# A second buffer for spilled S5 output matrices, and a ring of six instead of seven for the state input matrices

## The chip, the cores and the metric

The kernel runs on one core of one Trainium2 chip. Of that core's engines the text speaks of TensorE (PE in the profile, with PEld for its weight loads), VectorE (DVE), ScalarE (ACT), GpSimd (POOL) and SyncE (SP, which only issues DMAs here), and of its 16 DMA engines. The metric is the device time of one execution in microseconds; lower is better. 1.0 of a granted TensorE clock is 2.4 GHz, 0.5 is 1.2 GHz.

## The reference

One inference step of a trunk of four layers (S5, retention, Hyena, S5) at model width 1024, over 128 context tokens and 256 latent tokens (384 columns, T in the kernel). The part around the change is layer 0, a bidirectional S5 layer: 1024 channels in 64 groups of 16, each group driving one 64-dimensional complex diagonal state.

```python
proj = h @ w_in
u, gate = proj[..., :S5_WIDTH], proj[..., S5_WIDTH:]
for d in range(2):                       # both directions
    ab = exp(lam * dt)                   # complex, per state
    bu = einsum('blgh,gph->blgp', ud, bb)        # bb = f(lam, dt) * b
    h_t = ab * h_{t-1} + bu_t                    # associative scan
    yd = Re(einsum('blgp,ghp->blgh', h, c))
    y = y + yd
g = gelu(y + d_skip * u)
y = g * sigmoid(g @ w_glu + b_glu)
out = (y * silu(gate)) @ w_out
```

## The kernel before

**Chunked scan.** The scan is done in chunks of Q = 8 tokens. For every group and direction the kernel builds matrices from lam, b and c: a state input matrix (eight tokens of u into the state at the end of the chunk), a Toeplitz matrix (u to y inside the chunk), and an output matrix CP (state at the chunk's start into the eight y). Only the recurrence over 48 chunks is then sequential (`recur`, lines 770 to 799, on VectorE).

**Half blocks and blocks.** The 64 groups are sixteen half blocks hb of four groups; block b is the half blocks 2b and 2b+1 (128 channels). For layer 0 everything is generated in the kernel:

- `gen_b1` (line 642): loads b and c (`bc`, two half blocks a load), and on VectorE makes for each direction BP = F1 x b + FI x b' (`expand`, lines 626 to 636: two multiplies and an add, lines 631, 632 and 636). ScalarE then changes the sign of c in place (line 651).
- `gen_b2` (line 660): TensorE multiplies c with BP (line 668, the Toeplitz part, into a PSUM bank), and transposes BP (line 674, two PSUM banks). ScalarE copies the transposes to the tile PB (line 675), which is the transposed state input matrix of the half block, and the Toeplitz part to Kc (lines 677 to 680), which a DMA puts into HBM.
- `use_p(b)` (line 743, step P): TensorE multiplies U of the block with PB of its two half blocks (line 749); ScalarE copies to Ss (one buffer, line 751), TensorE transposes (line 758), ScalarE writes the chunk inputs X (line 761). With that the two PB buffers are free again.

All of these use the four PSUM banks of `psm`.

**Spilled output matrices.** CP of a half block is needed only later, behind the recurrence. Ten of the sixteen are generated there (`gen_c`). Six, hb in `SPL` = 4, 6, 8, 10, 12, 14, are generated early, in `gen_b1`, and spilled to HBM: for each direction VectorE writes CP (line 631) and the second product `xt` (line 632, tag `xs`, two buffers, so one half block's worth); an accumulating DMA adds `xt` to CP (line 634, issued by POOL); and when both have landed a DMA stores CP to `cpd` (line 650, on POOL's queue too). CP has one buffer of 4 KB per partition.

**Order.** The string PLAN0 gives the program order: A n generates half blocks until n exist, U n multiplies a slab of the input projection (two blocks of U), P n is `use_p`, T is a background unit (a slab of the modulation weights `mod_w`, 1 MB each), R0 and R1 are the recurrences of the first and second half of the blocks. R0 needs P0 to P3, R1 needs P4 to P7.

```python
PLAN0 = "A7 U0 T1 U1 T1 P0 A9 T1 P1 A11 T1 U2 T1 P2 A13 T1 P3 A15 T1 R0 U3 T1 P4 T1 A16 P5 T1 T1 P6 P7 R1"
```

The order that each engine really gets is fixed when the kernel is built: the framework lists instructions by their place in the program, simulates the engines, and issues on each the first one that is ready in its simulation. A tile that has no free buffer is not ready. So a number of buffers changes not only waits on the chip, but also the order in which instructions stand on the engines. On the chip each engine keeps that order.

**Behind it.** The gate half of the input projection (`dense`, line 141 matmuls, eight blocks) is held behind the last matmul of P7 (`issue_after(mark[0].ins)`). SP's queue also loads the Toeplitz matrices back (`Tt`, line 852). Pools are stacked, and when the pools of the generation are closed, the tiles of the next stage take their place: a new tile waits for the old tiles at the same addresses. Seven PB buffers lie at the start of that space; `sgate` covers the first three, the two `Tt` buffers the fourth and the fifth.

Of the kernel before, what the change touches and what calls it, by code (L numbers as in the profile page):

```python
# [10 lines left out]
F32 = mybir.dt.float32  # L11
# [20 lines left out]
LINE = 520  # L32
EHY = 2048
SPLIT = True
RB = 7
NBC = 2
NH = 2
RB1 = 10
# [69 lines left out]
def hybrid_trunk(ctx: ExitStack, tc: tile.TileContext, I, O, dbg=None, layers=(0, 1, 2, 3)):  # L108
# [518 lines left out]
    def expand(out, rot, T1, T2, x, sl, l0, bufs, eng, add, tag="xt"):  # L627
        c1 = T1[:, sl, l0:l0 + 4].rearrange("p e l -> p l e").unsqueeze(3).to_broadcast([128, 4, 8, 16])
        c2 = T2[:, sl, l0:l0 + 4].rearrange("p e l -> p l e").unsqueeze(3).to_broadcast([128, 4, 8, 16])
        t = rot.tile([128, 4, 8, 16], F32, tag=tag, name="xt", bufs=bufs)  # L630
        eng.tensor_tensor(out, c1, x[:, 0].unsqueeze(2).to_broadcast([128, 4, 8, 16]), op=OP.mult)  # L631
        eng.tensor_tensor(t, c2, x[:, 1].unsqueeze(2).to_broadcast([128, 4, 8, 16]), op=OP.mult)  # L632
        if add is None:
            nc.gpsimd.dma_start(out, t, accum_op=OP.add)
        else:
            add.tensor_tensor(out, out, t, op=OP.add)  # L636

    def expand_c(CP, rot, tb, xc, hb, xb, eng, add, tag="xt"):
        for d in range(2):
            expand(CP[:, d], rot, tb["B1"], tb["BI"], xc[:, d], slice(1, 9) if d == 0 else slice(8, 0, -1), d * 64 + hb * 4, xb, eng, add, tag)  # L640

    def gen_b1(j, hb, tb, rot, xb=1, nb=1, spill=False):
        if hb % nb == 0:
            tb["bc"] = rot.tile([128, nb, 2, 2, 2, 4, 16], F32, tag="bc", name="bc", bufs=2)
            (nc.gpsimd if hb > 2 else nc.sync).dma_start(tb["bc"], I["s5bc"][j, hb // 4, :, hb % 4:hb % 4 + nb])
        rb, xc = tb["bc"][:, hb % nb, 0], tb["bc"][:, hb % nb, 1]
        if spill:
            CP = rot.tile([128, 2, 4, 8, 16], F32, tag="CP", name="CP", bufs=1)
            expand_c(CP, rot, tb, xc, hb, 2, V, None, "xs")
            getattr(nc, SPQ).dma_start(I["cpd"][hb], CP.rearrange("p d g e c -> p (d g e c)"))  # L650
        S.activation(xc, xc, AF.Copy, scale=tb["sgn"][:, 1:2])
        BPs = []
        for d in range(2):
            BP = rot.tile([128, 4, 8, 16], F32, tag="BP", name="BP", bufs=2 if j else 3)
            expand(BP, rot, tb["F1"], tb["FI"], rb[:, d], slice(7, None, -1) if d == 0 else slice(0, 8), d * 64 + hb * 4, xb, V, G if j else V)
            BPs.append(BP)
        return BPs, xc
# [28 lines left out]

    def gen_c(j, hb, tb, rot, CP, xb, eng=V, add=G):
        xc = rot.tile([128, 2, 2, 4, 16], F32, tag="xc", name="xc")
        nc.sync.dma_start(xc, I["s5bc"][j, hb // 4, :, hb % 4, 1])
        expand_c(CP, rot, tb, xc, hb, xb, eng, add)  # L690

# [9 lines left out]
    def s5(i, j, nxt, begun=lambda: None):  # L701
        def mk(st, name, bufs=1, **kw):
            return st.enter_context(tc.tile_pool(name=f"{name}_{i}", bufs=bufs, reuse_waits="tile", **kw))
# [23 lines left out]
        eP = ExitStack()  # L727
        ring = mk(eP, "s5b", RB if j == 0 else RB1)
        ru = mk(eP, "s5a", 2)
# [5 lines left out]
        def get_p(hb):  # L735
            if j == 0:
                PBs[hb] = gen_b2(j, hb, tb, grot, gen_b1(j, hb, tb, grot, nb=NBC, spill=hb in SPL), ring)
            else:
                PBs[hb] = ring.tile([128, 4, 2, 128], F32, tag="PB", name="PB")
                PQ.dma_start(PBs[hb].rearrange("p g d c -> p (g d c)"), I["pbd"][hb])  # L740
# [194 lines left out]
    def retention(i, zpool, hpool, nxt):  # L935
# [44 lines left out]
        if True:  # L980
            todo = []
            grot = es.enter_context(tc.tile_pool(name="retgr", bufs=1, reuse_waits="tile"))
            tb = GEN[1]
            ops = {}

            def both(hb):
                if hb > 0:
                    gen_b2(1, hb - 1, tb, grot, ops.pop(hb - 1))
                if hb < 16:
                    ops[hb] = gen_b1(1, hb, tb, grot, xb=1)  # L990
                    gen_cs(1, hb, tb, grot)
            todo += [lambda hb=hb: both(hb) for hb in range(17)] + list(bg)
            bg.clear()
            for k, f in enumerate(todo):
                while len(bg) < S0 + k * (SLOTS - S0) // len(todo):
                    bg.append(lambda: None)
                bg.append(f)
# [580 lines left out]
```

## Time and profile before

| | us |
|---|---|
| runs shown | 1636.39, 1632.05, 1635.85 |
| their median | 1635.85 |
| profiled execution, its time | 1632.28 |
| profiled execution, its span | 1630.5 |
| mean granted TensorE clock | 0.951 |

| engine | busy us | share of the span |
|---|---|---|
| PE | 1449.2 | 89% |
| DVE | 1246.0 | 76% |
| ACT | 692.2 | 42% |
| POOL | 664.3 | 41% |

The span is the time from the first to the last instruction of the profiled execution; 1.8 us of its time lie around it. A share of busy time is a mean over stages; stages of S5 in layer 0 (to about 350 us), where TensorE has gaps, are read for themselves. A line of a timeline gives the start, the duration, the engine, the line in the code, the operation, output <- inputs, the count, and in brackets the idle time of the engine just before it, with what ended it.

### The profile page before, as it was taken

The page shows a single profiled execution, that of the slowest core. Times are in us where ns is not written, and L with a number is a line of the kernel's source. Part 1 is how long each engine was busy: PE and PEld are TensorE (multiplying, and loading weights), DVE is VectorE, ACT ScalarE, POOL GpSimd, SP SyncE. Part 2 cuts the span into 40 slices and gives each one's busy share as a digit, 9 for nine tenths or more (in the row PEclk, how much of TensorE's full clock was granted, in tenths as well). Part 3 has the DMA queues.
Part 4 walks back from the last instruction along what each step waited for, and adds up shares of the span by engine and source line. Part 5 has one row for each costly group of instructions (what it writes and reads, how often), then busy time and mean ns, then how long its engine had stood idle before and what let it go on. Part 6 is the DMA issues. An engine that isn't in the chain of part 4 may idle for free. (4 is left out here: it accounts for less than half of the span.)

```text
span 1630.5 us, 27608 instructions
## 1 busy us (share of the span) xinstructions
PE 1449.2 (89%) x10370; PEld 1280.7 (79%) x10370; DVE 1246.0 (76%) x2935; ACT 692.2 (42%) x1275; POOL 664.3 (41%) x484
## 2 busy tenths in 40 slices
PE   6778787798799899999979999999999999988996
PEld 3555585577588888889968988999998898767886
DVE  8966998699886767755968887888888874379565
ACT  2434522244333333334445544546445534542443
POOL 2111242325374857551225665655666332132221
PEclk9887899899799999999989999999999999999998
DMA  9487499843555555543333322322322345577531
GB/s 359 130 260 224 150 222 253 284 178 128 216 173 179 183 207 187 183 154 130 127 125 101 101 78 75 101 84 95 100 78 94 106 174 201 167 217 196 199 130 65
DMA packets 107805, 261.39 MB, mean 160 GB/s; under 512 B 28535, under 2 KB 68568, under 8 KB 88088
## 3 DMA queue, kind: packets, MB, share of 16 engines
q1 hardware_dynamic: 80768, 200.12, 37.2%
q0 software_dynamic: 11984, 34.87, 7.7%
q10 hardware_dynamic: 14920, 24.65, 4.3%
q8 instruction: 82, 1.34, 0.3%
q14 instruction: 51, 0.42, 0.1%
HBM read 220.37 MB, written 30.83 MB: 154 GB/s over the span
## 5 line engine op out<-in xcount | busy, mean ns | idle before, releaser
L136 POOL TENSOR_TENSOR wl<-wr,wh 128x1024 fp32r<-128x1024 f32 (+2 forms) x99 | 248.9, 2515 | 300.2 <-ACT wh L164 273.6
L164 ACT CAST wh<-wr 128x1024 fp32r<-128x1024 f32 (+4 forms) x211 | 215.7, 1028 | 315.0 <-PE psd L141 200.5
L141 PE MATMUL psd<-hh,wh 128*128 128x384 f32 x880 | 307.3, 350 | 13.5 <-DVE X L798 7.0
L141 PE MATMUL psd<-hl,wh 128*128 128x384 f32 x880 | 305.7, 347 | 6.4 <-DVE hl L472 6.2
L141 PE MATMUL psd<-hh,wl 128*128 128x384 f32 x880 | 305.3, 347 | 4.7 <-POOL wl L136 2.6
L151 DVE TENSOR_TENSOR wl<-wr,wh 128x1024 fp32r<-128x1024 f32 (+3 forms) x112 | 147.2, 1315 | 71.9 <-ACT wh L164 71.5
L141 PEld LDWEIGHTS psd<-hh,wh 128*128 128x128 f32 x880 | 169.7, 193 | 26.6 <-issue 14.5
L141 PEld LDWEIGHTS psd<-hl,wh 128*128 128x128 f32 x880 | 169.9, 193 | 15.9 <-DVE hl L472 8.9
L141 PEld LDWEIGHTS psd<-hh,wl 128*128 128x128 f32 x880 | 169.7, 193 | 12.2 <-issue 5.1
L141 PE MATMUL psd<-wl,hh 128*128 128x256 f32 x384 | 110.0, 288 | 4.0 <-POOL wl L136 2.0
L141 PE MATMUL psd<-wh,hh 128*128 128x256 f32 x384 | 110.0, 292 | 2.6 <-ACT k L1077 1.6
L141 PE MATMUL psd<-wh,hl 128*128 128x256 f32 x384 | 109.0, 286 | 0.0
L381 PE MATMUL psn<-wr,sgc 128*32 128x256 f32 x640 | 58.3, 460 | 35.0 <-DMA wr<-in_mod_w_dram 23.9
L141 PE MATMUL psd<-zb,wh 128*128 128x384 f32 x240 | 80.9, 338 | 0.0
L141 PEld LDWEIGHTS psd<-wl,hh 128*128 128x128 f32 x384 | 74.1, 193 | 6.3 <-POOL wl L136 3.2
L141 PEld LDWEIGHTS psd<-wh,hh 128*128 128x128 f32 x384 | 73.3, 193 | 4.5 <-ACT k L1077 2.0
L636 POOL TENSOR_TENSOR BP<-BP,xt 128x512 f32<-128x512 f32 x32 | 47.3, 1479 | 71.9 <-DVE xt L632 36.4
L141 PEld LDWEIGHTS psd<-wh,hl 128*128 128x128 f32 x384 | 74.1, 193 | 0.1
L631 DVE TENSOR_TENSOR CP<-B,xc 128x512 f32<-128x512 f32 x52 | 52.9, 1044 | 26.5 <-DMA scratch_cpd_dram<-CP 15.6
L632 DVE TENSOR_TENSOR xt<-BI,xc 128x512 f32<-128x512 f32 x52 | 47.2, 909 | 29.6 <-POOL CP L636 17.2
L381 PEld LDWEIGHTS psn<-wr,sgc 128*32 128x32 f32 x640 | 20.0, 124 | 56.9 <-DMA wr<-in_mod_w_dram 27.8
L797 DVE TENSOR_TENSOR X<-X,m 128x64 f32<-128x64 f32 x184 | 64.2, 349 | 0.0
(385 smaller groups left out, 3843.1 us busy)
## 6 DMA issues: line engine op xcount, KB each, us to landing
wr<-in_mod_w_dram SPq DMA_DIRECT2D x40, 1024.0 KB
wr<-in_hy_w_in_dram SPq DMA_DIRECT2D x32, 1024.0 KB
wr<-in_ret_w_in_dram SPq DMA_DIRECT2D x24, 1024.0 KB
wr<-in_s_w_in_dram SPq DMA_DIRECT2D x16, 1024.0 KB
wm<-in_mod_w_dram SPq DMA_DIRECT2D x8, 1024.0 KB
CP<-xt POOLq DMA_DIRECT2D x32, 256.0 KB, 7.2
Tt<-scratch_kd_dram SPq DMA_DIRECT2D x128, 64.0 KB
wr<-in_s_w_glu_dram SPq DMA_DIRECT2D x8, 1024.0 KB
```

Source lines behind the costliest of these rows:

```text
L136: G.tensor_tensor(out, a, b, op=op)
L141: TE.matmul(out, lhs[a], rhs[b], start=start and i == 0, stop=stop and i == len(combos) - 1)
L151: V.tensor_sub(out, a, b)
L164: S.copy(hi, ap)
L381: TE.matmul(ps[q * 32:(q + 1) * 32, :256], sg[:, kb, 6 - 2 * u:38 - 2 * u], raw[:, kb, :], start=u == 0 and k2 == 0, stop=u == 3 and k2 == 1)
L631: eng.tensor_tensor(out, c1, x[:, 0].unsqueeze(2).to_broadcast([128, 4, 8, 16]), op=OP.mult)
L632: eng.tensor_tensor(t, c2, x[:, 1].unsqueeze(2).to_broadcast([128, 4, 8, 16]), op=OP.mult)
L636: add.tensor_tensor(out, out, t, op=OP.add)
L797: V.tensor_add(dst, dst, m1[:, 0])
```

## The change

It gives the tile CP of the spilled half blocks (in `gen_b1`) two buffers in place of one, and the ring of PB tiles of layer 0 (`RB`, the pool `s5b`) six buffers in place of seven. A CP buffer and a PB buffer are both 4 KB per partition, so that the pools take the same space together. Nothing is computed otherwise; PLAN0, the `xs` pair of buffers and `SPL` stay.

```diff
@@ -32,7 +32,7 @@
 EHY = 2048
 SPLIT = True
-RB = 7
+RB = 6
 NBC = 2
@@ -645,7 +645,7 @@
         if spill:
-            CP = rot.tile([128, 2, 4, 8, 16], F32, tag="CP", name="CP", bufs=1)
+            CP = rot.tile([128, 2, 4, 8, 16], F32, tag="CP", name="CP", bufs=2)
             expand_c(CP, rot, tb, xc, hb, 2, V, None, "xs")
```

`RB` is used once: `ring = mk(eP, "s5b", RB if j == 0 else RB1)`.

## Rows read from the trace of the kernel before

**Rows 1.** The page: span, busy time by engine, and the chain by engine.

```profile
span 1630.5 us, 27608 instructions
PE 1449.2 (89%) x10370; PEld 1280.7 (79%) x10370; DVE 1246.0 (76%) x2935; ACT 692.2 (42%) x1275; POOL 664.3 (41%) x484
...
PE 8%; DVE 4%; ACT 1%; DMA 1%; issue 0%; POOL 0%; DVEq 0%; ACTq 0%; POOLq 0%
```

**Rows 2.** Busy time by stretch: PE, PEld, DVE, ACT, POOL; clock, DMA share, GB/s.

```profile
125.00:135.00 10.00, 10.00 (x80) 7.35 (x78) 7.96 (x14) 3.68 (x9) 0.56 (x1) 0.86 0.84 261
135.00:145.00 10.00, 10.00 (x89) 7.55 (x87) 6.56 (x13) 5.96 (x15) 2.87 (x4) 1.00 0.69 164
145.00:155.00 10.00, 3.56 (x42) 2.30 (x40) 3.54 (x8) 1.04 (x3) 0.52 (x1) 0.66 0.67 204
...
185.00:195.00 10.00, 8.66 (x102) 5.24 (x96) 10.00 (x84) 6.44 (x13) 0.56 (x1) 1.00 0.36 108
195.00:205.00 10.00, 10.00 (x70) 9.17 (x69) 8.03 (x51) 5.16 (x8) 2.25 (x1) 1.00 0.08 18
...
290.00:320.00 30.00, 22.28 (x250) 16.38 (x244) 18.60 (x46) 8.86 (x17) 10.62 (x10) 0.80 1.04 318
...
500.00:1000.00 500.00, 467.37 (x3207) 434.93 (x3206) 370.94 (x650) 219.23 (x427) 253.24 (x173) 0.98 0.43 144
```

**Rows 3.** Instructions of tile CP: its accumulating DMAs' issues, and times to landing.

```profile
L634 POOL DMA_DIRECT2D CP<-xt x32: 850/867/1256, 72.1 to 310.6; - x32
...
DMA to landing us min/median/max: 2.9/7.4/14.1
```

**Rows 4.** Timeline of DVE: the spilled matrices' writes, with the waits before them.

```profile
135.63 1.29 DVE L631 TENSOR_TENSOR CP<-B,bc 128x512 f32<-128x512 f32 x2 [2.54 <-DMA scratch_cpd_dram<-CP]
...
141.14 0.69 DVE L632 TENSOR_TENSOR xt<-BI,bc 128x512 f32<-128x512 f32 x1 [1.54 <-DMA CP<-xt]
...
143.71 0.69 DVE L632 TENSOR_TENSOR xt<-BI,bc 128x512 f32<-128x512 f32 x1 [1.27 <-DMA CP<-xt]
...
153.49 1.29 DVE L631 TENSOR_TENSOR CP<-B,bc 128x512 f32<-128x512 f32 x2 [6.46 <-DMA scratch_cpd_dram<-CP]
...
177.60 1.28 DVE L631 TENSOR_TENSOR CP<-B,bc 128x512 f32<-128x512 f32 x2
```

**Rows 5.** Timeline of PE: the two long waits of this stage.

```profile
156.25 1.94 PE L381 MATMUL psn<-wr,sgc 128*32 128x256 f32 x16 [6.60 <-DVE mod L393]
...
179.47 1.08 PE L668 MATMUL psm<-BP,bc 128*32 128x128 f32 x16 [8.49 <-ACT bc L651]
```

**Rows 6.** Timelines of PE and DVE: step P3, and the starts of R0 and R1.

```profile
162.91 1.95 PE L749 MATMUL psm<-PB,U 128*64 128x256 f32 x16
...
168.95 0.18 DVE L778 COPY XF<-X 128x32 f32<-128x32 f32 x1 [0.55 <-ACT X L761]
...
201.84 0.18 DVE L778 COPY XF<-X 128x32 f32<-128x32 f32 x1 [1.97 <-ACT X L761]
```

**Rows 7.** Timelines of ACT (PB copies of hb 8, 12, 14), PE (P1, P4).

```profile
125.82 0.58 ACT L675 COPY PB<-psm 128x512 f32<-128x512 f32 x1 [0.61 <-PE psm L674]
...
162.58 1.07 ACT L675 COPY PB<-psm 128x512 f32<-128x512 f32 x2 [0.15 <-PE psm L674]
...
181.64 0.58 ACT L675 COPY PB<-psm 128x512 f32<-128x512 f32 x1 [0.61 <-PE psm L674]
...
126.57 1.62 PE L749 MATMUL psm<-PB,U 128*64 128x256 f32 x8
...
182.38 1.95 PE L749 MATMUL psm<-PB,U 128*64 128x256 f32 x16
```

**Rows 8.** Timelines of SP (Toeplitz and weight loads) and PE (P7's second half).

```profile
189.26 5.69 SPq L852 DMA_DIRECT2D Tt<-scratch_kd_dram  x8
206.64 0.34 SPq L155 DMA_DIRECT2D wr<-in_mod_w_dram  x1
...
194.82 1.08 PE L749 MATMUL psm<-PB,U 128*64 128x256 f32 x8
```

## Prediction, made before the result was known

> **What bounds the kernel now.** I first read the page. TensorE is busy 89% of the span, and the chain that ended last has only 8% of PE and 4% of DVE on it, since it reaches back no further than the last layer [rows 1]. It therefore says nothing about layer 0, where the change is, and I follow the waits there by hand.
>
> Next I read the busy time by stretch. In the middle of the kernel PE works 467.37 of 500 us [rows 2]: there a stage that starts earlier ends as much earlier, since the work before its end is fixed. Around 150 us it is otherwise: between 145 and 155 us PE works 3.56 us of 10, DVE 3.54, ACT 1.04, POOL 0.52 [rows 2]. Every engine stands still together, so one wait holds them all. The timeline of DVE names it: at 153.49 the write of a spilled CP had waited 6.46 us for the store of the CP before it [rows 4]. There is one CP buffer, so the next may be written only when the store has read the last. PE's next work had then waited 6.60 us for a DVE instruction that stands behind that write [rows 5]. The same wait, 2.54 us, stands before the write at 135.63 [rows 4]. The other writes show next to none of it.
>
> Then I ask whether that time reaches the end. The half blocks made on DVE feed P3 on PE at 162.91, its X lets R0 start on DVE at 168.95, R1 starts at 201.84 when P7's X is there [rows 6]; the gate's matmuls are held behind P7. Between them DVE is full (10.00 us of 10 from 185 to 195) [rows 2]. So a microsecond that DVE gains before 160 us moves R0, and with it R1 and the gate. The stretch behind, 290 to 320 us, has its DMA engines full (share 1.04), but they do nearly nothing (0.08) between 195 and 205 us [rows 2]: those loads wait for buffers that the gate's matmuls free, so they move forward together with P7.
>
> **The second CP buffer.** It removes the two waits for the store: 2.54 + 6.46 = 9.0 us of DVE time, both before P3 and with no other work of DVE beside them [rows 4]. In their place may come the wait for the `xs` pair, which keeps two buffers: the products of the next spilled half block wait until the accumulating DMAs have read the last ones. This is seen as 1.54 and 1.27 us at 141.14 and 143.71 [rows 4]. But those accumulates were issued behind the CP write at 135.63; if CP is written some 6 us earlier, beside its products, they land earlier too. Bounds: the pair's waits vanish (2.8 us more gain), or they grow until they replace the removed waits (the gain is 0). I take them as they are, 2.8 us, nearest to the rows that show them.
>
> The last spilled matrix, half block 14, is written at 177.60 without a wait, because the order fixed at build time put it there, within R0; PE had then waited 8.49 us for ACT's sign change, which needs that write done [rows 4, 5]. With a free buffer the planner can put it where its products stand, before R0. That lets P4 to P7 end earlier, but R1 also needs R0's end, and R0 is bound by DVE. I count nothing for it; its bound above is the 1.97 us that DVE waited before R1 [rows 6]. No instruction is added: six matrices with their writes, accumulates and stores stay. What moves on POOL's queue is the accumulate's issue, 0.87 us each, two a matrix [rows 3], and the store, which waits in that queue until both have landed; the loads of `bc` stand in that queue too, and would wait 1.7 us for a pair moved ahead of them. They are prefetched a pair of half blocks ahead, which hides that; uncovered it costs 1.7 us.
>
> At one place a rule speaks against this. What the rows show is a DMA share of 0.84 between 125 and 135 us, against 0.69 in the ten microseconds after it, where these accumulates run now [rows 2]; and times to landing of 7.4 us at the median, 14.1 at most [rows 3]. Moved earlier, they go into the fuller stretch. The Trainium skill, page "DMA: Bandwidth & Descriptors", section "Issuing engines are not separate DMA queues", says that DMAs of all issuing engines run on the same 16 engines and interleave. By that rule a second matrix in flight gains no bandwidth of its own, and the result is the second rival below; the rows bear it out only as far as the landing times vary.
>
> **Six PB buffers.** Half block n can now be copied into PB only after the matmuls that read half block n-6, instead of n-7. I lay ACT's copies beside the P steps. Half block 8 is copied at 125.82 and would wait for the first half of P1, which ends at 126.57 + 1.62 = 128.2: 2.4 us. Half block 12 is copied at 162.58 and would wait for P3's first half, 162.91 + 1.95/2 = 163.9: 1.3 us. Half block 14 at 181.64 waits for P4's first half, 182.38 + 1.95/2 = 183.4: 1.7 us [rows 6, 7]. Half block 10 is like half block 12, and the odd ones are copied after the other half, so they don't wait; nor does half block 6, copied after P0's first half. What is queued behind a waiting copy is ACT's own work (Kc, the sign of c, Ss), and two of the four `psm` banks are held meanwhile. The P steps are near the copies, since nothing but the order keeps them back: their U and their PB are there long before. Of the four only half block 12's lies in front of R0, as its two copies may now come between P3's matmuls and P3's Ss. I charge 1.3 us. Bounds: 0, if ACT's order lets Ss go first, and the four waits in full, 4 x 2.4 = 9.6 us.
>
> The six buffers also move what lies over them. `Tt`'s first buffer will lie where the last half blocks were, so its load, now at 189.26, can wait until P7's matmuls are over at 194.82 + 1.08 = 195.9: 6.6 us later [rows 8]. It takes 5.69 us to issue, so it would be done by 201.6, and SP's next load, of `mod_w`, goes out only at 206.64, when a weight buffer comes free [rows 8]. That slack of 5 us hides it, and P7 moves forward besides; without the cover, up to 6.6 us of delay would reach the weight loads queued behind it on SP. I count nothing.
>
> **Sum.** -9.0 + 1.3 = -7.7 us. Against the profiled execution: 1632.28 - 7.7 = 1624.6 us. That execution lies 3.6 us under the median of the runs shown, 1635.85, so I expect a median of 1628.2 us.
>
> **Rivals.** (1) More is gained: the pair's waits go (2.8) and so does the wait before R1 (1.97), and the ring costs nothing: 9.0 + 2.8 + 2.0 = 13.8 us, 1622. For it: the late write at 177.60 held PE for 8.49 us. Against it: R0 has DVE to itself.
> (2) The place of the wait is taken: the second buffer is there, but the `xs` pair holds the next matrix, as two accumulates land in up to 14.1 us and not 7.4. Then 6.7 of the 9.0 us come back, and with the ring's 1.3 the gain is 1.0: 1635, no change. For it: the pair's waits are in the rows already, and the DMA share is high. Against it: the removed wait comes after an accumulate *and* a store, one landing after the other; the pair's waits for the accumulate alone.
> (3) The ring closes, and it is slower. The place is ACT's copy to PB. If the planner makes half blocks 9 us earlier, but leaves P3 and P4 where they are (162.91 and 182.38), then half blocks 12 and 14 each wait 9.0 us more in front of ACT's queue, with two PSUM banks held. This costs 2 x 9.0 against 9.0 gained: 9 us slower, 1645. It decides from the point where P steps move less than the half blocks do; A stands ahead of P in PLAN0, so the order prefers to make half blocks. Against it: P needs nothing but a bank and its turn.
> (4) The new order disturbs a later stage, in either sign; the trace of before can't show it. I let it widen the range by some 3 us.
>
> **How the numbers follow.** Forecast 0.42, rival 1 0.12, rival 2 0.26, rival 3 0.15, rival 4 0.05. A run of this kernel can tell about 0.3% from no change, 4.9 us: faster means below 1631, slower above 1640.8. The forecast and rival 1 are faster but for a tenth of the forecast that ends short: 0.50. Rival 2, that tenth and a part of 4 are the same: 0.32. Rival 3 and the rest are slower: 0.18. Cases of both signs matter; the forecast's own range is 1624 to 1631 (the pair's waits, and the ring at 0 to 4 us). For 8 in 10 I take 1619, which is rival 1 less 3 us, to 1643, which cuts off the upper half of rival 3.
>
> **What would show it.** Right: no wait of DVE for the store of CP; CP and its products side by side; the stretch 145 to 155 us filled; P3, R0 and R1 each some 8 us earlier, and the same distance still there at 500 us. Ring: ACT's copies to PB behind line 749, by 1 to 2 us. Wrong: long waits of line 632 for an accumulate (rival 2); copies to PB that wait several microseconds, with P3 no earlier than 162 (rival 3); or R1 earlier and the end not, which would mean that the stretch at full DMA share gives the gain back.

## The result, and the profile of the changed kernel

| | before | changed |
|---|---|---|
| median, us | 1635.85 | 1647.93 |
| lowest and highest, us | 1630.1 to 1637.31 | 1643.74 to 1655.2 |
| time of the profiled execution, us | 1632.28 | 1647.11 |
| its span, us | 1630.5 | 1645.2 |

The ratio is 1.0086, 95% interval 1.0057 to 1.0116: slower, by about 14 us by that ratio (the two medians differ by 12.1). 1628.2 was forecast, and 1643 was the upper end of the range.

The page of the changed kernel, as [rows 1]: the busy time of every engine is that of before within 5 us. PE's own time for the same 10370 matmuls is 4.6 us longer (its mean granted clock is 0.946, before 0.951); the rest of the 14.7 us of span is time in which it waits.

```profile
span 1645.2 us, 27617 instructions
PE 1453.8 (88%) x10370; PEld 1285.2 (78%) x10370; DVE 1245.1 (76%) x2935; ACT 691.9 (42%) x1275; POOL 662.0 (40%) x484
...
PE 7%; DVE 5%; DMA 1%; ACT 0%; SPq 0%; issue 0%; POOL 0%; DVEq 0%; ACTq 0%; POOLq 0%
```

The same stretches as in [rows 2] (busy us of PE, PEld, DVE, ACT, POOL; granted clock, DMA share, GB/s). Between 145 and 155 us, where every engine had stood still, PE now works 8.21 us and DVE 7.94: that hole is gone. But from 290 to 320 us PE works 16.93 us where it had 22.28.

```profile
125.00:135.00 10.00, 10.00 (x81) 7.52 (x78) 8.37 (x16) 4.75 (x10) 2.74 (x4) 0.93 0.97 269
...
145.00:155.00 10.00, 8.21 (x112) 5.15 (x108) 7.94 (x18) 4.25 (x11) 1.11 (x2) 1.00 0.99 288
...
290.00:320.00 30.00, 16.93 (x158) 12.32 (x159) 19.07 (x40) 6.10 (x10) 11.47 (x11) 0.72 0.92 296
500.00:1000.00 500.00, 467.78 (x3191) 434.44 (x3191) 364.45 (x634) 215.96 (x425) 250.79 (x172) 0.97 0.43 144
```

DVE's timeline, as [rows 4] and [rows 6]: the spilled writes (CP<-B,bc), the starts of R0 and R1 (XF<-X), the first CP of the Y stage (CP<-B,xc) and the last xT of layer 0. No write waits for a store; two wait for the load of `bc` instead. R0 starts 5.2 us earlier than in [rows 6], R1 3.9 us earlier. Then it turns: Y's first CP comes at 235.37 (before: 224.93), and the last xT of layer 0 at 418.83 (before: 412.00). The changed kernel first, then the last two of these for the kernel before.

```profile
126.56 1.29 DVE L631 TENSOR_TENSOR CP<-B,bc 128x512 f32<-128x512 f32 x2
140.27 0.69 DVE L631 TENSOR_TENSOR CP<-B,bc 128x512 f32<-128x512 f32 x1 [3.29 <-DMA bc<-in_s5bc_dram]
...
158.22 0.69 DVE L631 TENSOR_TENSOR CP<-B,bc 128x512 f32<-128x512 f32 x1 [2.48 <-DMA bc<-in_s5bc_dram]
...
163.71 0.18 DVE L778 COPY XF<-X 128x32 f32<-128x32 f32 x1 [1.07 <-ACT X L761]
...
197.93 0.18 DVE L778 COPY XF<-X 128x32 f32<-128x32 f32 x1 [4.19 <-ACT X L761]
...
235.37 0.68 DVE L631 TENSOR_TENSOR CP<-B,xc 128x512 f32<-128x512 f32 x1
...
418.83 0.74 DVE L522 SCALAR_TENSOR_TENSOR xT<-psd,gt,xT 128x128 f32<-128x128 f32 x2 [3.81 <-PE psd L141]
```

```profile
224.93 0.67 DVE L631 TENSOR_TENSOR CP<-B,xc 128x512 f32<-128x512 f32 x1
...
412.00 0.74 DVE L522 SCALAR_TENSOR_TENSOR xT<-psd,gt,xT 128x128 f32<-128x128 f32 x2 [3.81 <-PE psd L141]
```

What stands ahead of that first CP is found on SP's timeline, as [rows 8]. Its input `xc` is loaded at 226.42, behind 32 Tt loads (8 + 5 + 9 + 5 + 5). Before (second fence), it stood behind 16, the 8 of [rows 8] and 3 + 5 more, and was loaded at 214.30.

```profile
192.06 6.15 SPq L852 DMA_DIRECT2D Tt<-scratch_kd_dram  x8
...
203.13 3.20 SPq L852 DMA_DIRECT2D Tt<-scratch_kd_dram  x5
...
210.11 6.59 SPq L852 DMA_DIRECT2D Tt<-scratch_kd_dram  x9
...
217.37 3.49 SPq L852 DMA_DIRECT2D Tt<-scratch_kd_dram  x5
221.47 0.33 SPq L155 DMA_DIRECT2D wr<-in_s_w_in_dram  x1
221.84 4.32 SPq L852 DMA_DIRECT2D Tt<-scratch_kd_dram  x5
226.42 0.85 SPq L689 DMA_DIRECT2D xc<-in_s5bc_dram  x2
```

```profile
207.03 1.82 SPq L852 DMA_DIRECT2D Tt<-scratch_kd_dram  x3
...
209.59 4.39 SPq L852 DMA_DIRECT2D Tt<-scratch_kd_dram  x5
214.30 0.81 SPq L689 DMA_DIRECT2D xc<-in_s5bc_dram  x2
```

### The profile page after: what moved, and what is told of

It is laid out like the page before. It is cut to its first block, busy times and chain, and to the rows that moved or that the text cites. A ratio compares the mean times of both kernels' runs of the same rounds, so it can differ in the third digit from the quotient of the medians.

```text
span 1645.2 us, 27617 instructions
## 1 busy us (share of the span) xinstructions
PE 1453.8 (88%) x10370; PEld 1285.2 (78%) x10370; DVE 1245.1 (76%) x2935; ACT 691.9 (42%) x1275; POOL 662.0 (40%) x484
## 5 line engine op out<-in xcount | busy, mean ns | idle before, releaser
L151 DVE TENSOR_TENSOR wl<-wr,wh 128x1024 fp32r<-128x1024 f32 (+3 forms) x112 | 146.7, 1310 | 70.7 <-ACT wh L164 70.5
L381 PE MATMUL psn<-wr,sgc 128*32 128x256 f32 x640 | 57.1, 446 | 34.5 <-DMA wr<-in_mod_w_dram 30.6
L636 POOL TENSOR_TENSOR BP<-BP,xt 128x512 f32<-128x512 f32 x32 | 47.0, 1470 | 53.4 <-DVE xt L632 22.3
L632 DVE TENSOR_TENSOR xt<-FI,bc 128x512 f32<-128x512 f32 x64 | 49.6, 775 | 19.9 <-POOL BP L636 10.7
L381 PEld LDWEIGHTS psn<-wr,sgc 128*32 128x32 f32 x640 | 19.5, 121 | 55.5 <-DMA wr<-in_mod_w_dram 28.7
```

Of the source, the lines that this page charges most:

```text
L151: V.tensor_sub(out, a, b)
L381: TE.matmul(ps[q * 32:(q + 1) * 32, :256], sg[:, kb, 6 - 2 * u:38 - 2 * u], raw[:, kb, :], start=u == 0 and k2 == 0, stop=u == 3 and k2 == 1)
```

## The experiments

Three theories. **Theory 1**: the time is lost behind R1, in the Y stage (the stage that writes the other CPs and makes y), since the planner's new order puts the `xc` loads behind twice as many Tt loads. **Theory 2**: the smaller ring costs it, since Tt's buffers now lie over the last half blocks' PB. **Theory 3**: any edit gives a new plan, and the later stages come out by chance. Later a question was added about the stage ahead of R1.

One table serves all runs. Each row is a profiled execution, cut at the start of R1, at the start of the last xT of layers 0, 1 and 2, and at the end; all cells but the last two are us of that one execution. "Ratio" is the kernel's time against the kernel before on the same chip, with its interval. The rows were measured on several chips, on which the kernel before had medians from 1631.5 to 1635.9, so kernels are compared by the ratio and not by the median.

| kernel (label) | R0 starts | R1 starts | R1 to end of layer 0 | layer 1 | layer 2 | layer 3 | median us | ratio |
|---|---|---|---|---|---|---|---|---|
| before | 168.9 | 201.8 | 210.2 | 415.8 | 554.8 | 247.9 | 1635.85 | 1 |
| before, again (e5) | 160.9 | 194.1 | 212.2 | 415.2 | 556.0 | 246.5 | | |
| changed | 163.7 | 197.9 | 220.9 | 420.8 | 555.7 | 249.9 | 1647.93 | 1.0086 |
| changed, again (e6) | 165.1 | 200.7 | 220.7 | 418.9 | 555.0 | 249.9 | | |
| ring of six alone (e1) | 176.9 | 209.3 | 211.5 | 417.5 | 555.0 | 247.9 | 1642.63 | 1.0052 (1.0025 to 1.0079) |
| the same, again (e12) | 174.6 | 206.5 | 213.9 | 419.1 | 554.3 | 247.2 | | |
| the same, third (e18) | 172.7 | 205.0 | 214.7 | 417.8 | 555.8 | 249.7 | | |
| changed, pools swapped (e2) | 164.1 | 197.6 | 212.9 | 417.6 | 558.8 | 247.8 | 1644.29 | 1.0069 (1.0036 to 1.0101) |
| the same, again (e7) | 164.7 | 197.7 | 214.0 | 421.4 | 558.6 | 255.2 | | |
| changed, swapped in layer 0 (e11) | 167.9 | 200.6 | 213.3 | 419.6 | 557.9 | 252.8 | 1643.53 | 1.0071 (1.0050 to 1.0092) |
| before, pools swapped (e8) | 173.4 | 207.6 | 218.5 | 417.1 | 558.0 | 254.8 | 1653.39 | 1.0108 (1.0073 to 1.0143) |
| changed, `xc` by ACT (e3) | 166.3 | 199.3 | 215.6 | 419.0 | 557.4 | 248.1 | 1643.37 | 1.0069 (1.0040 to 1.0097) |
| before, `xc` by ACT (e4) | 167.5 | 200.6 | 217.1 | 419.5 | 554.6 | 248.9 | 1641.73 | 1.0050 (1.0021 to 1.0080) |
| changed, `xc` behind 16 Tt (e9) | 165.8 | 200.3 | 210.5 | 414.6 | 555.0 | 247.8 | 1634.93 | 1.0019 (1.0000 to 1.0037) |
| before, `xc` behind 32 Tt (e10) | 166.5 | 202.7 | 214.4 | 417.4 | 555.8 | 250.4 | 1641.85 | 1.0055 (1.0031 to 1.0079) |
| changed, `xc` behind 8 Tt (e16) | 164.2 | 197.0 | 218.4 | 416.9 | 557.8 | 248.7 | 1640.45 | 1.0040 (1.0017 to 1.0064) |
| before, `xc` behind 8 Tt (e17) | 165.1 | 198.1 | 216.0 | 418.4 | 556.8 | 249.5 | 1646.11 | 1.0083 (1.0057 to 1.0108) |
| e9 with four `bc` buffers (e13) | 183.2 | 210.4 | 211.8 | 416.3 | 555.7 | 247.1 | 1646.59 | 1.0103 (1.0072 to 1.0135) |
| before with four `bc` buffers (e14) | 177.0 | 201.1 | 220.6 | 416.3 | 555.3 | 244.5 | 1649.78 | 1.0118 (1.0089 to 1.0147) |
| e9 with `bc` by SP (e15) | 165.7 | 198.4 | 212.4 | 413.5 | 557.3 | 249.0 | 1636.43 | 1.0032 (1.0007 to 1.0058) |

**The same kernels again (e5, e6, e7).** No edit.

> The kernel before, unchanged, profiled a second time, for the size of what moves between two executions of one kernel. If the 10 to 15 us between the two kernels come from their orders, then the second trace shows each milestone (R1's start at 201.8, the last gate at 252.2, xT of layer 0 at 412.3, of layer 1 at 828.0) within some 3 us of the first. If executions of one kernel scatter, these milestones move by 5 us or more.

> The changed kernel, unchanged, profiled a second time. Theory 1: R1 starts at about 198 us again, Y's first matrix is written at about 235 us again, and xT of layer 0 ends near 419 us: the loss in the Y stage is in the order and returns. If it was chance, xT of layer 0 ends at 405 to 412.

> The changed kernel with the two pools in the other order, profiled a second time; its twelve times lie between 1633.7 and 1650.6, the first profile was of one near the lower end (1636.45). Theory 1: the early gain of 4 us still stands at 340 us, and what varies from execution to execution arises behind it. Theory 3: the early milestones vary too.

Behind R1, two executions of one order agree within 2 us in each stretch, for the kernel before and for the changed one (others spread more: the ring alone 3.2 us from R1 to the end of layer 0, the swapped kernel 3.8 in layer 1 and 7.4 in layer 3). Ahead of it they don't: R0 of the kernel before came at 168.9 and at 160.9 us. The second execution's spilled writes show why. The wait of 6.46 us at 153.49 [rows 4], the largest term of the forecast, is 1.24 us here:

```profile
134.03 1.30 DVE L631 TENSOR_TENSOR CP<-B,bc 128x512 f32<-128x512 f32 x2 [2.34 <-DMA scratch_cpd_dram<-CP]
...
146.89 1.29 DVE L631 TENSOR_TENSOR CP<-B,bc 128x512 f32<-128x512 f32 x2 [1.24 <-DMA scratch_cpd_dram<-CP]
...
165.80 1.29 DVE L631 TENSOR_TENSOR CP<-B,bc 128x512 f32<-128x512 f32 x2 [0.18 <-DMA scratch_cpd_dram<-CP]
```

So the gain of 5 us at R0 that one pair of traces shows is no gain of the change: against this second trace the changed kernel's R0 is 2.8 us late. The loss from R1 to the end of layer 0 is in the order: 210.2 and 212.2 us before, 220.9 and 220.7 changed.

**The ring alone (e1, e12, e18).** The changed kernel with one CP buffer, which is the kernel before with `RB = 6`:

```diff
-            CP = rot.tile([128, 2, 4, 8, 16], F32, tag="CP", name="CP", bufs=2)
+            CP = rot.tile([128, 2, 4, 8, 16], F32, tag="CP", name="CP", bufs=1)
```

> Ring of six half blocks, one buffer for the spilled matrix: the second part of the change alone. Theory 1 (the time is lost in layer 0's Y stage, where the loads of `xc` stand behind 32 Tt loads of SP's queue instead of 16): this kernel's order has 16 Tt loads ahead of the first `xc`, as before, so Y's first matrix is written at about 225 to 228 us, not 235, and the time is that of before or the ring's 1 to 3 us above it, 1633 to 1640. Theory 2 (the ring itself costs it, by the Tt buffers that now lie under the last half blocks): Tt's first load starts at P7's end, and the time is some 10 us above before, about 1645. Theory 3 (any edit makes a new plan, and the later stages come out by chance): the early part is as before, and offsets of several us either way arise at the later stages, of another size and at other places than in the changed kernel.

> The ring of six alone, profiled a second time. In its first profile the last gate came at 259.9 us (before: 252.2 and 244.3; changed: 247.0 and 249.5), and all behind took as long as before but for 2 us. If the ring itself costs the P stage some 10 us, which the second CP buffer then only buys back, the last gate comes at 256 to 262 again; if it was that execution, at 244 to 253.

> The ring of six alone, a third profile, for R0's start. If the ring costs the P stage 5 us or more, R0 starts at 172 to 178 us again and the last gate comes at 256 to 261. If the two profiles so far were late by chance, R0 starts at 161 to 170.

It is slower by 0.52%, about 8.5 us, and not for theory 2's reason. Tt's first load does start as late as it can, at 203.42 us in e1, behind P7; yet from R1 to the end of layer 0 it takes 211.5 to 214.7 us, in the mean 2 us more than the kernel before and 7 less than the changed one. What is late is R0: 172.7 to 176.9 us, where six executions of the kernel before's order up to R0 (before, e4, e5, e8, e10, e17) have 160.9 to 173.4, mean 167.1. The mean of the three is 174.7: 7.7 us later (R1: 206.9 against 200.8, 6.1 later). Not all of it is the ring's: at P0's first half, up to which the traces of the two kernels have the same order on every engine, the three executions already are 2.6 us behind the mean of the six (108.7 against 106.1). The order on PE shows a likely cause of some of the rest. First PE of the ring alone (e12), then of the kernel before's order (e10, where line 749 is 752): P0's two halves, and a matmul of the mod vectors (L381) that waits for its weights.

```profile
108.85 1.08 PE L749 MATMUL psm<-PB,U 128*64 128x256 f32 x8
118.85 1.93 PE L381 MATMUL psn<-wr,sgc 128*32 128x256 f32 x16 [8.92 <-DMA wr<-in_mod_w_dram]
120.72 1.98 PE L749 MATMUL psm<-PB,U 128*64 128x256 f32 x8
```

```profile
108.10 1.08 PE L752 MATMUL psm<-PB,U 128*64 128x256 f32 x8
110.36 1.08 PE L752 MATMUL psm<-PB,U 128*64 128x256 f32 x8 [1.17 <-ACT PB L675]
...
117.62 1.93 PE L381 MATMUL psn<-wr,sgc 128*32 128x256 f32 x16 [6.18 <-DMA wr<-in_mod_w_dram]
```

The plan for six buffers puts the mod matmul ahead of P0's second half. Its weights are late in both (it starts at 118.85 and 117.62), so P0's second half starts 10 us later; by P1 the ring alone is 3.6 us behind in the mean. The changed kernel has the same order there, but in the eight traces of its order the mod matmul started at 112.7 to 115.4 us, and P0's second half 1.9 us behind it. How much of the 7.7 us this order makes was not measured by itself.

**Where Tt lies (e2, e11, e8).** The pools `ru` and `ring` are made in the other order, in both S5 layers (e2; e8 on the kernel before) or in layer 0 alone (e11). No instruction is added or removed; only addresses are edited, and the order behind R1 follows from them:

```diff
-        ring = mk(eP, "s5b", RB if j == 0 else RB1)
         ru = mk(eP, "s5a", 2)
+        ring = mk(eP, "s5b", RB if j == 0 else RB1)
```

> The changed kernel with the two pools `ru` and `ring` made in the other order, so that Tt's buffers no longer lie over the last half blocks' PB. SP's order then has 16 Tt loads ahead of the first `xc`, as before the change. Theory 1: R1 stays 4 us earlier than before, Y's first matrix is written at about 220 to 225 us, the 12 us lost between 240 and 345 us come back, and the time is 1628 to 1637. Theory 2: the same, since the overlay is gone too. Theory 3: the loss moves elsewhere, and the time is anywhere between 1630 and 1650.

> The changed kernel with the pools `ru` and `ring` swapped in layer 0 alone. With the swap in both S5 layers the stretch from the last gate to the end of layer 0 took 160.8 and 161.9 us, but the last layer 247.5 and 254.9 (246 to 248 before). Theory 1: the gain of 10 us in layer 0 stays, and without the swap in the last layer the time is 1634 to 1640. Theory 3 (any new plan loses somewhere behind): 1641 to 1648 again.

> The kernel before with nothing changed but the order in which the two pools `ru` and `ring` are made: seven PB buffers and one CP buffer, other addresses. No instruction is added or removed and the order up to R1 is the same; behind R1 the plan differs. Theory 1 and theory 2: no reason for a loss, 1629 to 1636. Theory 3 (the order of before is a lucky one, and any other plan of the same work costs some 8 to 12 us behind R1): 1640 to 1646.

On the changed kernel the swap moves `xc` ahead of 16 of the Tt loads, and R1 to the end of layer 0 takes 212.9 to 214.0 us, 7 to 8 less. The time hardly follows: 1.0069 and 1.0071, as layers 1 to 3 together take 6 to 17 us longer than in the kernel before (e2: 417.6 + 558.8 + 247.8 against 415.8 + 554.8 + 247.9). On the kernel before, the same swap costs 1.08%, some 18 us, though its order up to R1 is unchanged: R1 to the end of layer 0 takes 218.5 us and layer 3 254.8. This is theory 3's sign, and larger than it expected.

**`xc` by another queue (e3, e4).**

```diff
-        nc.sync.dma_start(xc, I["s5bc"][j, hb // 4, :, hb % 4, 1])
+        (nc.sync if j else nc.scalar).dma_start(xc, I["s5bc"][j, hb // 4, :, hb % 4, 1])
```

> The changed kernel, with layer 0's `xc` loads of line 689 issued by ACT instead of SP, so that no Tt load stands ahead of them in their queue; placement unchanged. Theory 1: Y's first matrix is written at 225 us or before and the Y stage ends some 10 us earlier than in the changed kernel: 1633 to 1640. Theory 2 (the overlay of Tt holds the Y stage, not `xc`): Tt's loads are as late as in the changed kernel and the time stays at 1644 to 1650. Theory 3: no relation, 1635 to 1655.

> The kernel before with the same edit as the run above (`xc` of layer 0 issued by ACT). It tells what that edit does by itself. Theory 1: before, `xc` stood behind 16 Tt loads only and Y's first matrix was written at 224.93 us, so little is to be won: 1632 to 1637. Theory 2: no change either. Theory 3: a shift of several us at the later stages, of either sign.

On the changed kernel it gains 5 us in the Y stage (215.6), on the kernel before it loses 5 to 7 (217.1). It tells little: with this edit both orders come out at about the same place, 1.0069 and 1.0050, and their intervals overlap.

**The order pinned (e9, e10).** e9 emits the first two `xc` loads before the third Tt and ties that Tt's loads behind them. On the kernel before, this pin changes nothing in the built order, as the expectation below has it; it was not run there. e10 ties the kernel before's `xc` loads behind the last load of the fourth Tt.

```diff
         for m in range(TMB):
+            if m == 2 and j == 0:
+                for hb in (0, 2):
+                    XC[j, hb] = load_xc(j, hb, rot)
             toeplitz(m)
...
+                with tc.issue_after(xcl[0].ins) if j == 0 and m == 2 else ExitStack():
                     nc.sync.dma_start(Tt[16 * t:16 * t + 16], src)
```

> The changed kernel, placement and instructions untouched, with one order pinned: the first two `xc` loads of layer 0's Y stage are issued ahead of the third Tt's eight loads, so 16 Tt loads stand ahead of them on SP's queue and not 32 (in the kernel before the same pin changes no row of any engine). Measured so far, from the last gate to the end of layer 0 (last xT): before 160.1 and 162.2 us, changed 172.0 and 171.8. Theory 1 (`xc` behind the Tt loads costs the Y stage its 10 us): 160 to 163 us here, and the time falls by about 10 to 1634 to 1640. Theory 2 (Tt's place over the last half blocks' PB costs it): 170 to 173 us still, and 1644 to 1650.

> The kernel before with the opposite pin: layer 0's `xc` loads are issued behind the last load of the fourth Tt, so 32 Tt loads stand ahead of them, as in the changed kernel; seven PB buffers, one CP buffer, placement untouched, order up to R1 the same. Theory 1: from the last gate to the end of layer 0 it takes about 170 us instead of 161, and the time is 1640 to 1646. Theory 2: 160 to 163 us, and 1629 to 1637.

The pin gives the changed kernel the whole loss back: 210.5 us from R1 to the end of layer 0, layer 1 in 414.6, 1634.93 us, ratio 1.0019 (e13 and e15 below, which carry the same pin, have 211.8 and 212.4 in that stretch). The other pin costs the kernel before 2 to 4 us there, not the 10 that theory 1 asked for, and 0.55% in all, though Y's first CP comes at 245.7, later than in any other run. Nor does an early one help: with `xc` by ACT it comes at 204.3 (e3) and 202.5 (e4), and the stretch takes 215.6 and 217.1 us. So theory 1 fails in its simple form: the start of Y's first CP doesn't set the end of the layer.

What PE waited for is seen in its waits for DMAs between 235 and 345 us (total us, times, longest). The kernel before, then the changed one, then the changed one pinned (e9, where line 857 is 868 and line 884 is 898):

```profile
PE psn L381 <- DMA wr<-in_mod_w_dram: 12.3, 5, 4.9
...
PE psm L857 <- DMA Tt<-scratch_kd_dram: 1.9, 2, 1.0
PE psm L884 <- DMA CP<-xt: 0.3, 1, 0.3
```

```profile
PE psn L381 <- DMA wr<-in_mod_w_dram: 11.7, 4, 5.7
PE psm L884 <- DMA CP<-xt: 8.1, 3, 5.1
PE psm L857 <- DMA Tt<-scratch_kd_dram: 6.8, 2, 4.4
```

```profile
PE psn L381 <- DMA wr<-in_mod_w_dram: 6.4, 3, 5.9
...
PE psm L898 <- DMA CP<-xt: 4.1, 3, 3.1
...
PE psm L868 <- DMA xc<-in_s5bc_dram: 3.4, 1, 3.4
```

In sum 14.5, 26.6 and 13.9 us: 12.1 more in the changed kernel and the same again when pinned, beside 10.7 more and 0.3 more us of the stretch (210.2, 220.9, 210.5). The changed order's second trace has 27.2, e10 18.7. The new waits are for accumulates of CP and for Tt, while the DMA engines are full. The windows of 240 to 260 us show it: before, changed, pinned.

```profile
240.00:260.00 20.00, 14.11 (x124) 11.94 (x124) 19.81 (x117) 1.94 (x4) 3.82 (x5) 0.84 0.90 248
```

```profile
240.00:260.00 20.00, 7.18 (x59) 3.39 (x57) 16.73 (x87) 0.86 (x2) 5.14 (x6) 0.65 1.06 272
```

```profile
240.00:260.00 20.00, 13.59 (x99) 10.53 (x98) 17.55 (x105) 1.35 (x3) 3.45 (x4) 0.84 1.05 253
```

The DMA share is as high when pinned (1.05) as without (1.06), so the share alone doesn't make the loss. What the pair doesn't settle: the pin also made the planner move other work (the two traces' orders part at 216 us on DVE and at 231 on PE, and differ in many places behind), so the order as a whole is shown to be the cause, and the place of `xc` in it only as what sets that order off.

**Earlier still (e16, e17).** The same pin one Tt earlier: 8 Tt loads ahead of `xc`.

> The changed kernel with the first two `xc` loads ahead of the second Tt: 8 Tt loads before them in SP's queue, where the pinned version had 16 (1634.9 us; 157.2 us from the last gate to the end of layer 0) and the changed kernel 32 (1647.9; 172). Theory 1, if the first CP of Y is still what the stage waits for: another 2 to 4 us, 1630 to 1634, and the stretch takes 154 to 157 us. If with 16 the transposes of the Tt are what Y waits for: no further gain, 1634 to 1638 and 157 to 162 us. Theory 3: the new plan loses it elsewhere, 1638 to 1646.

> The same in the kernel before: 8 Tt loads ahead of the first `xc` where it had 16. Theory 1, first form: 1628 to 1632, and 156 to 160 us from the last gate to the end of layer 0 (160.1 and 162.2 before). Second form: 1630 to 1636. Theory 3: 1636 to 1646, with the loss at stages behind layer 0.

No gain by degrees: 1.0040 and 1.0083, with 218.4 and 216.0 us from R1 to the end of layer 0. In e17 PE waits 11.6 us for accumulates of CP between 235 and 345 us. In e16 it waits only 7.7 us for DMAs there, less than in any kernel of the fences above, and the stretch is long all the same: its longest wait, 9.3 us, is for DVE (`mod`, line 393). So each order loses its time at another wait. By the medians the order with 16 is better than those with 8 and with 32.

**What took the place of the store (e13, e14, e15).** All three on the pinned order. e13 (changed) and e14 (before) load `bc` by half block into four buffers, e15 (changed) loads it by SP:

```diff
-NBC = 2
+NBC = 1
...
-            tb["bc"] = rot.tile([128, nb, 2, 2, 2, 4, 16], F32, tag="bc", name="bc", bufs=2)
+            tb["bc"] = rot.tile([128, nb, 2, 2, 2, 4, 16], F32, tag="bc", name="bc", bufs=2 if j else 4)
```

```diff
-            (nc.gpsimd if hb > 2 else nc.sync).dma_start(tb["bc"], I["s5bc"][j, hb // 4, :, hb % 4:hb % 4 + nb])
+            nc.sync.dma_start(tb["bc"], I["s5bc"][j, hb // 4, :, hb % 4:hb % 4 + nb])
```

> The changed kernel with the pinned `xc` order, and `bc` loaded by half block into four buffers instead of by pairs into two (same memory, same bytes). A half block's load can then start one half block earlier. Theory A (the wait for `bc` took the place of the wait for the store and holds R1): DVE's waits for `bc` of 5 to 8 us shrink to under 3, R0 and R1 start 3 to 6 us earlier (R1's first product at 197 to 200 us, against 204.0), and the time falls from 1634.9 to 1629 to 1632. Theory B (R1 is held by the P steps on PE): R1 stays at 201 to 204, and the time at 1633 to 1637.

> The same four `bc` buffers in the kernel before (its order of `xc` is the pinned one already). Theory A: with one CP buffer the waits for the store stay (5 to 9 us in sum) and little is won: 1630 to 1635, no faster than before by more than 2 us. Theory B: no change either, 1630 to 1635.

> The changed kernel with the pinned `xc` order, `bc` in its two buffers, but all its loads issued by SP, so that none stands behind accumulates or a store in POOL's queue. Theory A, if it is the place in POOL's queue that makes `bc` late: its waits shrink to under 3 us and R1 comes 3 to 6 us earlier, 1629 to 1632. If it is the buffer (the load can't be issued before the half block two pairs back is done): the waits stay at 5 to 8 us and the time at 1633 to 1638. Theory B: R1 unchanged in either case.

None of the three is faster, but they don't refute theory A (the wait for `bc` holds R1): each edit replaced the order ahead of R0 as well. In e13 the wait for `bc` is down to 1.05 us between 90 us and R1, and R0 starts at 183.2, 17 us later than in e9; but P0, too, starts only at 118.39, where e9 has 107.32. In e14 the waits for the store sum to 2.33 us between 125 and 200, and yet it is 1.18% slower, where both theories saw no change. In e15 DVE's waits are as long, only elsewhere (the spilled writes):

```profile
113.05 0.69 DVE L631 TENSOR_TENSOR CP<-B,bc 128x512 f32<-128x512 f32 x1 [5.95 <-DMA bc<-in_s5bc_dram]
...
138.98 0.69 DVE L631 TENSOR_TENSOR CP<-B,bc 128x512 f32<-128x512 f32 x1 [2.70 <-DMA bc<-in_s5bc_dram]
```

The traces of the changed order itself say more, and not on DVE. On ACT, the sign change of the last pair's `bc` (line 651) stands ahead of half block 12's copies to PB and of P3's Ss. It waits for that pair's load, which POOL issues right behind a store of CP. POOL, then ACT, of the changed kernel:

```profile
148.77 0.56 POOL L650 DMA_DIRECT2D scratch_cpd_dram<-CP  x1 [4.82 <-DVE BP L636]
149.34 0.55 POOL L645 DMA_DIRECT2D bc<-in_s5bc_dram  x1
```

```profile
158.15 0.51 ACT L651 ACTIVATE bc<-bc,sgn 128x256 f32<-128x256 f32 x1 [3.96 <-DMA bc<-in_s5bc_dram]
158.57 1.05 ACT L675 COPY PB<-psm 128x512 f32<-128x512 f32 x2
159.51 1.08 ACT L751 COPY Ss<-psm 128x512 f32<-128x512 f32 x2
```

In the eight traces of this order ACT waits 1.67 to 5.42 us there; the sign change starts at 158.2 to 162.2 us, and R0 follows 5.1 to 6.3 us behind it each time. So the load of `bc` does stand in R0's path. It isn't all that does: in e15 the sign change waits for nothing, but P3 starts 3.1 us later than in e9, and R0 comes at the same time (165.7; 165.8 in e9). What the wait for `bc` costs the kernel in all was not measured with the order kept.

No version was found that beats the kernel before; the nearest is e9, whose interval begins at 1.0000. The second CP buffer with seven PB buffers was not tried.

## Why the prediction was wrong, by its own steps

**The sum at R1.** Forecast -7.7 us. Over the executions that share an order up to R0, R0 starts at 167.1 before (six) and 165.2 changed (eight: changed, e2, e3, e6, e7, e9, e11, e16); R1 at 200.8 and 198.9. So the gain is 1.9 us, less than the spread of one kernel (12.5 us at R0 before, 4.2 changed). It is made of two parts: P3's first matmul comes 3.9 us earlier in the mean (159.7, then 155.9), and from there to R0 it takes 2.0 us longer (7.4, then 9.4).

**The second buffer, -9.0.** Mechanism right, size wrong: no DVE write waits for a store, and none for the `xs` pair either, which the forecast kept at 2.8 us. The term was read from one execution. The waits for the store between 125 and 200 us sum to 9.00 in it, but to 3.76 (e5), 4.59 (e8), 4.24 (e10), 4.12 (e17) and 4.77 us (e4) in the others of the same order; 6.46 of the 9.00 were one store that landed late. In their place stand DVE's waits for `bc`, 1.59 to 7.73 us in sum in the changed order's traces. Beside the ring of six, R0 comes 9.5 us earlier with the buffer (174.7 to 165.2), R1 8.0. That this is near the -9.0 is in part luck: at P0's first half the executions with the ring alone are already 2.8 us behind those of the changed order (108.7 and 105.9), two of the three with at most 0.8 us of store waits ahead of it.

**The wait for `bc`, 1.7 "uncovered".** The prediction put it at nothing, since the loads are prefetched a pair ahead. It came, and not only on DVE: ACT waits 1.67 to 5.42 us for the last pair's load, with P3's Ss behind it. In the seven traces with 3.5 us or more of this wait, P3 to R0 takes 8.9 to 11.2 us; in e6, with the 1.67, it takes 6.6. (Before, it takes 4.9 to 6.0 in four traces, and 10.2 and 11.2 in the two where ACT waits 4.0 and 6.7 us for a store of Kc.)

**The ring, +1.3.** The wait came as foreseen: in the three traces of the ring alone, half block 12's copies wait 0.88 to 1.24 us for P3's first half. But the ring alone is 7.7 us late at R0 and 6.1 at R1, within its own bound of 9.6; 2.6 of it stood there before the orders part, and the order of the mod matmul before P0's second half was not foreseen. The bounds were worked out on the old order, and the edit made a new one.

**What is late next at R1.** Ahead of R1 DVE waits 1.87 to 4.18 us for P7's X before, and 2.58 to 4.58 changed (4.19 in the first trace, against 1.97 in [rows 6]). R1 follows R0 by 33.7 us in the mean before and by 33.6 changed, so R1 gains what R0 gains.

**Tt over the last half blocks, 0.** Near enough. The load starts at 192.06, when P7's last matmul is over, and the ring alone, which has the same overlay, takes 211.5 to 214.7 us from R1 to the end of layer 0, against 210.2 and 212.2.

**"They move forward together with P7".** The step that cost most. It took the stages behind R1 to be the old ones, shifted. They were planned anew: R1 to the end of layer 0 takes 9.6 us longer (means of two traces each: 211.2 and 220.8), layer 1 takes 4.4 and layer 3 2.7 longer. Less the 1.9 us gained at R1 that is 14.8 us, near the measured 14. The prediction named this as its rival 4, "in either sign", gave it 3 us and a chance of 0.05. The pin shows that the order makes it. Where the order was left alone the step holds: from 460 to 1470 us the two kernels' traces have the same order on every engine; layer 1's loss is there by 520 us, and from there to the end of the layer the changed kernel stays 14.9 to 15.5 us behind (means of two traces each); layer 2 takes the same time (555.4 us both). The last sentence of the prediction's signs, R1 earlier and the end not, is what came; its reason, the full DMA share, isn't enough, as the pinned kernel has that share without the loss.

**Rival 2 and its rule.** No write of the P stage waited for an accumulate, so a second matrix in flight did not put that wait in the store's place. The Trainium skill's rule cited there (page "DMA: Bandwidth & Descriptors", section "Issuing engines are not separate DMA queues") says that DMAs run on the same 16 engines whichever engine started them. e15 is in line with it, as waits of 5.95 and 2.70 us for `bc` are left after its move to SP; no run measured the bandwidth by itself.

## What to carry to other kernels

Where a planner orders all engines at build time, an edit of buffer counts or of addresses can replace the order of stages far behind it, so "the rest moves as a whole" is a claim of its own: compare the built orders of all engines behind the change, and expect the old times only where the order is the old one. The place of one load was no measure of the loss here. Read a wait that is to be removed in two or more executions before it enters a sum; a long DMA landing can be that execution's alone. And ask of every engine, not only of the one that waited, which load will be late next. Keep a control that changes no work, as the swapped pools were here, to learn what a new order alone costs: every kernel here whose order behind R1 differs from the kernel before's was slower in the median, by 0.2 to 1.2% (the 0.2%, e9, is at the edge of its interval).

## What the runs showed of the hardware

Executions of one order differ early. Between 50 and 60 us, after ten microseconds in which PE had worked 4.80 and 4.39 us, the granted clock was 0.80 in one execution of the kernel before's order (e5) and 0.52, near the lower level of 1.2 GHz, in another (e8), and PE got through 70 and 53 matmuls:

```profile
50.00:60.00 10.00, 9.13 (x70) 5.73 (x70) 10.00 (x23) 8.47 (x21) 0.00 (x0) 0.80 0.33 107
```

```profile
50.00:60.00 10.00, 9.20 (x53) 6.50 (x54) 10.00 (x23) 8.51 (x21) 0.00 (x0) 0.52 0.31 107
```

R0 came at 160.9 in the first and at 173.4 in the second. At the first spilled write the second was only 1.2 us behind (69.5 and 70.7), so most of the distance arises later; one part is seen on ACT ahead of R0, where the second waits 3.95 us for a store of Kc and the first doesn't. How much of the 12.5 us is the clock's and how much the DMAs' was not separated.
